# A two-layer trunk on one core: part of product yt4 between the context transposes and the latent kv product, a norm over four transpose banks, sums issued in steps

## The chip, the cores and the metric

The kernel runs on one core of one Trainium2 chip. The metric is the device time of the program in microseconds (us), lower is better. Engines: TensorE does the matmuls (PE) and loads their weights (PEld); VectorE (DVE), ScalarE (ACT) and GpSimd (POOL) work on rows and tiles; SyncE (SP), ACT and POOL also issue DMAs, each on a queue of its own.

## The reference, cut to what matters

A trunk of two layers over 256 latent tokens and 256 context tokens, model width 1024, all in f32. Layer 0 mixes tokens with a bidirectional chunkwise mLSTM, layer 1 with multi-head latent attention in which the latents read context and latents. Behind each mixer follows a gated feed-forward with a depthwise convolution over time. Every sub-layer ends in a LayerNorm and the next begins with a modulation (scale and shift from the condition):

```python
x = _layer_norm(ALPHA * x + ml[2] * yl, ln_g[i, 0], ln_b[i, 0])
f = _conv_ffn(_modulate(x, ml[3], ml[4]), ffn_w_in[i], ffn_conv_w[i], ffn_conv_b[i], ffn_w_out[i])
x = _layer_norm(ALPHA * x + ml[5] * f, ln_g[i, 1], ln_b[i, 1])
...
# latent attention, keys and values, for context (ang None) and latents
ckv, k_rope = jnp.split(h @ w_dkv, [A_KVLORA], axis=-1)
kv = (_rms_norm(ckv, kv_norm) @ w_ukv).reshape(B, T, A_HEADS, A_DNOPE + A_DV)
# queries, for latents only
q = (_rms_norm(h @ w_dq, q_norm) @ w_uq).reshape(B, T, A_HEADS, A_DNOPE + A_DROPE)
```

In layer 1 the context is only read: no output and no feed-forward of the context is computed there.

## The kernel before

**Numbers in two halves.** Every f32 operand is split into a high part in fp32r (an ACT cast) and a low part (a DVE subtraction, operand minus high part). `mm3` (L384 to L386) makes one product of three matmuls: high x high, high x low, low x high. In a product of activations with weights, L385 is the one that reads the low half of the weights, L386 that of the activations.

**The weights' stream.** `Stream` brings all weights in one fixed order, that of `_plan`. `_load` issues the DMA of a weight tile (512 KB at full width) into a ring of buffers called raw, on SP's queue. `_split` makes the ACT cast (L323) and the DVE subtraction (L326). Most halves go to one of three buffers w, and a split waits until PE has released one; weights marked wide go to the large pool u instead (tile wu), and need no release. A raw buffer comes free when its low half is made, and the load that takes its place is issued then.

**The output product of the first feed-forward** (`w_fout0`) is a Strassen-Winograd scheme: seven products of quarter size instead of eight, with sums around them. Four of them, yt2, y11, yt3, yt1, run interleaved over six weight tiles each, into pairs of PSUM banks p6, p1, p7, p5. Then DVE and ACT form the sums of these banks: u2 = p6 + u2 (L1437), p7 = p7 + u2 (L1439), v = p5 - p7 (L1443), p5 = p5 - u2 (L1444), each for two banks. Then y21 accumulates on p1, y22 on p5, yt4 on p7, six weight tiles each, the sixth of half width. The weights of yt4 are made by two transfers: a load from t2d, where sums of other weights have been kept (L278, SP), and on top of it an accumulating DMA from the weights (L279, POOL).

The context rows are complete before yt4. They are normalised (`z_norm`), transposed on PE (`ln_T`, L1197, tile zT), modulated (tile zm, L1204 on ACT, L1206 on DVE) and split (L1209, L1210) into hc, while the first three tiles of yt4 run. Then comes the context's kv product (`mla_ctx`, tile dkv), and then the last three tiles of yt4 (`YTAIL = 3`, marked wide), first for bank 0, then for bank 1. Behind these the latents are normalised the same way, between the context's keys and values (kn, v1).

**Latent attention** (`mla`) begins with the latents' kv product (dkv), the query's down-projection (dq), an rms norm of both (`rms`: square, sqrt and reciprocal, and the scaling L1513 on DVE), transposes, and so on. `ln_x` multiplies the latent rows with gain and bias (L1225, L1226 on DVE) and stores them for the next residual; it waits in the list `late` until `take_late` moves it to the background work.

**The second feed-forward** (layer 1) begins with `after0`: `ln_rows`, then `ln_T`, then the input product (fin). `ln_T` takes one PSUM bank for two of eight 128-column blocks, with both row tiles; of a pair, the first block is modulated by ACT and, where `tail` holds, the second by DVE.

**The order of the work.** Python generators in `bg` hold background work; `tick(n)` runs n steps of it between matmul groups, `drain` the rest. This is the program order; the framework's scheduler then fixes the order on each engine by its own estimate of when operands are ready, except where `keep_in_program_order` pins an instruction. Each engine executes its list in order, and waits on semaphores.

Of the kernel before, what the change touches and what calls it, by code (L numbers as in the profile page):

```python
# [10 lines left out]
AF = mybir.ActivationFunctionType  # L11
ALU = mybir.AluOpType
# [19 lines left out]
NB, NRAW, NU, NS = 3, 3, 31, 15  # L32

SUMS = 5

AHEAD = 8
QA, QB, QC = 2, 4, 6
# [19 lines left out]
YTAIL = 3  # L57
# [13 lines left out]
def _plan():  # L71
    ids, order = {}, []

    def add(key, cols, wide=False):
        if key not in ids:
            ids[key] = (len(ids), cols)
        order.append((key, wide))

    for m in range(16):
        add(("up", m, 0), 1024)  # L80
    for s in range(4):
        for c in range(4):
            add(("og", s, c), 1024)
    for p in range(2):

        for j in range(4):
            for n in ("vt2", "v11", "vt3", "vt1"):
                add((n, p, j), 1024)
        for j in range(4):
            for n in ("v21", "vt4", "v22"):  # L90
                add((n, p, j), 1024)
    add(("gates", 0, 0), 256)
    for h in range(H0):
        for j in range(4):
            for c in range(2):
                add(("qk", (h * 2 + j) if j < 2 else (8 + h * 2 + j - 2), c), 1024)
    for g in range(2):
        for k in range(16):
            add(("mout", 0, k), 1024, g == 1 and k >= 16 - WIDE["mout"])
    for p in range(NF):  # L100
        add(("fin0", p, 0), 1024)
        add(("fin0", p, 1), 1024)
    cols = [1024] * 5 + [512]
    for j in range(6):
        for n in ("yt2", "y11", "yt3", "yt1"):
            add((n, 0, j), cols[j])
    for n in ("y21", "y22", "yt4"):
        for j in range(6):
            if (n, j) == ("yt4", 6 - YTAIL):
                for c, m in enumerate((3, 3, 2)):  # L110
                    add(("dkv", 0, c), m * 320)
            add((n, 0, j), cols[j], n == "yt4" and j >= 6 - YTAIL)
    for c in range(2):
        add(("ukn", 0, c), 1024, True)
    for c in range(2):
        add(("uv", 0, c), 1024, True)
    for c in range(4):
        add(("dq", 0, c), 768)
    for c, n in enumerate((2, 1)):
        add(("uqr", 0, c), n * 512)  # L120
    for c in range(3):
        add(("uqn", 0, c), 1024)
    for k in range(8):
        add(("aout", 0, k), 1024, k >= 8 - WIDE["aout"])
    for p in range(NF):
        add(("fin1", p, 0), 1024, p < 2)
        add(("fin1", p, 1), 1024, p < 2)
    for k in range(NF):
        add(("fout1", 0, k), 1024, k >= NF - WIDE["fout1"])
    return ids, order  # L130
# [224 lines left out]
class K:  # L355
# [830 lines left out]
        nc.vector.tensor_tensor(B, B, sh, op=ALU.add)  # L1186
        return A, B

    def ln_T(self, zs, A, B, dst, tail):

        nc = self.nc
        for kp in range(4):
            pt = self.ps("zT")
            for i in range(2):
                k = kp * 2 + i
                for t in range(2):
                    nc.tensor.transpose(pt[:, i * 256 + t * 128:i * 256 + (t + 1) * 128],  # L1197
                                        zs[t][:, k * 128:(k + 1) * 128], self.ident)
            tmp = self.s2("zm")
            for i in range(2):  # L1200
                k = kp * 2 + i
                c = slice(i * 256, (i + 1) * 256)
                if i == 0 or not tail:
                    nc.scalar.activation(tmp[:, c], pt[:, c], AF.Identity, bias=B[:, k:k + 1], scale=A[:, k:k + 1])  # L1204
                else:
                    nc.vector.tensor_scalar(tmp[:, c], pt[:, c], A[:, k:k + 1], B[:, k:k + 1],  # L1206
                                            op0=ALU.mult, op1=ALU.add)
                hi, lo = dst(k)
                nc.scalar.copy(hi, tmp[:, c])  # L1209
                nc.vector.tensor_sub(lo, tmp[:, c], hi)  # L1210
                if not tail and i == 0:
                    yield
            yield

    def ln_x(self, ln, zs, dst):

# [146 lines left out]
    def w_fout0(self, x1d, mid):  # L1363


        nc, st, A = self.nc, self.st, self.fa
        pin = self.tc.keep_in_program_order
# [4 lines left out]
        def operand():  # L1372
            if parts:
                x, i = parts.pop(0)
                r = self.s2("zr")
                js = [j for j in (2 * i, 2 * i + 1) if j < 11]
                for h, j in enumerate(js):
                    pin(nc.scalar.dma_start(r[:, h * 256:(h + 1) * 256], self.fd[j][:, off[x]:off[x] + 256]))
                got.append((x, js, r))
            if len(got) > 2 or not parts and got:  # L1380
                x, js, r = got.pop(0)
                n = 256 * len(js)
                u = self.u("fz")
                pin(nc.scalar.copy(u[:, 0, :n], r[:, :n]))
                nc.vector.tensor_sub(u[:, 1, :n], r[:, :n], u[:, 0, :n])
                for h, j in enumerate(js):
                    A[x, j] = u[:, :, h * 256:(h + 1) * 256]
# [13 lines left out]
        lo, hi = slice(0, 512), slice(512, 1024)  # L1401
        p6, p1, p7, p5 = [pair() for _ in range(4)]
        n = 0
        u2 = []
        for i in range(6):
            for name, ps, x in (("yt2", p6, "S2"), ("y11", p1, "1"), ("yt3", p7, "S3"), ("yt1", p5, "S1")):
                w = st.use((name, 0, i))
# [8 lines left out]
                if n == 14:  # L1416
                    gate = []
                    for g in (1, 0):
                        t = self.uf("gate")
                        nc.gpsimd.dma_start(t, self.gd[0, 5][g:g + 1, :].to_broadcast([128, 1024]))  # L1420
                        gate.append(t)
                if n >= 16 and n % 2 == 0:
                    if n == 16:
                        z = []
                    t = self.uf("z")
# [7 lines left out]
                        u2.append(u)  # L1433
        stats = [self.tiny(12, "st").rearrange("p (a b) -> p a b", b=6) for _ in range(4)]
        vv = []
        for b in range(2):
            nc.vector.tensor_tensor(u2[b], p6[b], u2[b], op=ALU.add)  # L1437
        for b in range(2):
            nc.vector.tensor_tensor(p7[b], p7[b], u2[b], op=ALU.add)  # L1439
        for b in range(2):  # L1440
            v = self.s2("v")
            nc.scalar.copy(v, p7[b])
            nc.vector.tensor_tensor(v, p5[b], v, op=ALU.subtract)  # L1443
            nc.vector.tensor_tensor(p5[b], p5[b], u2[b], op=ALU.subtract)  # L1444
            vv.append(v)

        def add(g, c, ps, bs=(0, 1)):

            for b in bs:
                t = self.s2("zp")  # L1450
                zz = z[2 * g + b][:, c]
                nc.vector.tensor_tensor(t, ps[b], gate[g][:, c], op=ALU.mult)
                nc.vector.scalar_tensor_tensor(zz, zz, ALPHA, t, op0=ALU.mult, op1=ALU.add)
                nc.vector.bn_stats(stats[2 * g + b][:, c.start // 512], zz)

        def last():
            for b in range(2):
                add(1, hi, vv, (b,))
                yield

        for i in range(6):
            w = st.use(("y21", 0, i))
            prod(p1, "2", w, i, on=True)
            self.tick(1)
            operand()
        add(0, lo, p1)
        self.bg.append(last())
        for i in range(6):
            w = st.use(("y22", 0, i))
# [7 lines left out]
        for i in range(6 - YTAIL):  # L1477
            w = st.use(("yt4", 0, i))
            prod(p7, "3", w, i, on=True)
            self.tick(2)  # L1480
        self.drain()
        mid(None, None, None)
        ws = [(i, st.use(("yt4", 0, i), hold=True)) for i in range(6 - YTAIL, 6)]
        for b in range(2):
            for i, w in ws:
                prod(p7, "3", w, i, (b,), True)
        st.unhold("yt4")
        self.fa = self.fd = None
# [18 lines left out]
    def rms(self, ps, n, dst):  # L1507
        nc = self.nc
        ss = self.tiny(1, "rs")
        nc.scalar.activation(dst, ps, AF.Square, accum_out=ss)  # L1510
        nc.scalar.activation(ss, ss, AF.Sqrt, bias=self.keps, scale=1.0 / n)
        nc.vector.reciprocal(ss, ss)
        nc.vector.tensor_scalar(dst, ps, ss, None, op0=ALU.mult)  # L1513

    def rope_rows(self, out, src, t, n):

# [107 lines left out]
    def mla(self, hl):  # L1624
        nc, st = self.nc, self.st
# [1 line left out]
        rows = self.dkv_rows(self.dkv_mm(hl, self.wd), 2)  # L1627
        self.wd = None
        st.unhold("dkv")
        self.tick()  # L1630
        pss = [self.ps("dq0"), self.ps("dq1")]
        for c in range(4):
            w = st.use(("dq", 0, c))
# [157 lines left out]
def build(tc, off, a, out):  # L1791
    es = ExitStack()
    with es:
        k = K(tc, es, off, a)
        nc = k.nc
# [54 lines left out]
        def after0(pss, xr, gate, g, ln, l, c, dst, xdst):  # L1850
            cond = 1 - g
            A, B = k.ln_mod_cols(ln, l, c, cond)
            yield from k.ln_rows(pss, xr, gate)
            zs = k.zs
            yield from k.ln_T(zs, A, B, dst, g == 1)
            if xdst is not None:
                k.late.append(k.ln_x(ln, zs, xdst))

# [38 lines left out]
        def norm1(g, zs, stats, first):  # L1897
            A, B = k.ln_mod_cols(1, 1, 0, 1 - g)
            if first is not None:
                first()  # L1900
                hlu.extend([k.u("hl") for _ in range(4)])
            yield from k.z_norm(zs, stats)
            yield from k.ln_T(zs, A, B, hl if g else hc, g == 1)
            if g:
                k.late.append(k.ln_x(1, zs, [x2d[0], x2d[1]]))
        k.w_fout0(x1d, mid)
# [8 lines left out]
        k.tick(4)  # L1915
        k.uv((1,))
        k.drain()
        k.take_late()
        att = k.mla(hl)
        oT = next(att)  # L1920
        hl = hlu = None
# [54 lines left out]
```

## Time and profile before

| | |
|---|---|
| median of 3 runs | 1380.56 us (1380.09 to 1381.29) |
| profiled execution: device time | 1379.68 us |
| its span | 1377.9 us |
| granted TensorE clock | 0.998 |
| PE, PEld busy | 1349.8 us (98%), 1121.5 us (81%) |
| DVE, ACT, POOL busy | 1074.9 us (78%), 719.8 us (52%), 121.4 us (9%) |
| HBM read, written | 262.90 MB, 33.46 MB |

The stages that the diff touches lie between 1000 and 1190 us of the span. Where PE pauses there is best read by stage (time stretches of 10 us; busy us and instruction count of each engine, then the granted clock, the mean busy share of the 16 DMA engines, and GB/s):

```profile
1000.00:1010.00 10.00, 8.15 (x35) 5.83 (x34) 10.00 (x15) 8.31 (x12) 0.00 (x0) 1.00 0.90 305
...
1040.00:1050.00 10.00, 9.18 (x59) 7.96 (x58) 6.53 (x21) 9.00 (x22) 3.35 (x5) 1.00 1.04 264
...
1070.00:1080.00 10.00, 8.86 (x51) 7.76 (x52) 9.94 (x23) 7.44 (x19) 0.21 (x1) 1.00 0.00 0
1080.00:1090.00 10.00, 9.04 (x55) 8.69 (x54) 9.49 (x22) 4.96 (x11) 1.96 (x4) 1.00 0.75 241
...
1180.00:1185.00 5.00, 2.63 (x19) 2.01 (x18) 3.72 (x12) 3.11 (x9) 0.00 (x0) 1.00 0.00 0
```

The columns behind the length are PE, PEld, DVE, ACT and POOL. The first row holds the sums of `w_fout0`, the second the context's transposes and its kv product, the third and fourth the latents' transposes, kv product and dq, the last the norm ahead of the second feed-forward. A line of the trace names an instruction by its line, engine, operation and tiles, with the time that its engine sat idle before it and what ended that wait in brackets.

### The profile page before, as it was taken

To read this page: it belongs to the slowest core of one execution; us is meant where nothing else is said; L and a number is where in the kernel's file an instruction comes from. 1 tells how busy PE (TensorE), PEld (TensorE's weight loads), DVE (VectorE), ACT (ScalarE), POOL (GpSimd) and SP (SyncE) were. 2 spreads that over 40 slices of the span, in tenths; PEclk is the share of its full clock that TensorE was granted. 3 is DMA by queue.
4 is the path that set the end of the run, shared out by engine and by line. 5 is a ranking of instruction groups with operands and counts; after the bars stand their busy time and mean duration, and the time that the engine had idled before them with its cause. 6 is when DMAs were issued, how large, how long until landed. Compare 5 with 4: busy or idle time off the path is not lost.

```text
span 1377.9 us, 18614 instructions
## 1 busy us (share of the span) xinstructions
PE 1349.8 (98%) x6583; PEld 1121.5 (81%) x6583; DVE 1074.9 (78%) x1744; ACT 719.8 (52%) x1238; POOL 121.4 (9%) x215
## 2 busy tenths in 40 slices
PE   7999999999999999999999999999999999999997
PEld 3788888888788888878798888888878888888886
DVE  6599757677588696878789977767888889888873
ACT  6585434445544455364644334334557667466660
POOL 0032000011001011120001000000001001000100
PEclk9999999999999999999999999999999999999999
DMA  9689848789666363766747877746887435356760
GB/s 339 232 294 323 284 153 252 236 288 300 215 196 212 108 230 118 255 194 227 234 139 252 291 243 228 220 144 204 304 252 251 150 100 204 111 185 186 253 201 31
DMA packets 97900, 297.58 MB, mean 216 GB/s; under 512 B 12136, under 2 KB 24808, under 8 KB 97808
## 3 DMA queue, kind: packets, MB, share of 16 engines
q1 hardware_dynamic: 68672, 218.52, 48.7%
q0 software_dynamic: 17472, 57.57, 13.2%
q10 hardware_dynamic: 11664, 20.32, 4.1%
q8 instruction: 51, 0.84, 0.3%
q14 instruction: 41, 0.34, 0.1%
HBM read 262.90 MB, written 33.46 MB: 215 GB/s over the span
## 4 chain that ended last, share of the span: by engine, by line
PE 89%; DVE 5%; ACT 2%; DMA 2%; issue 1%; SPq 0%; ACTq 0%; DVEq 0%
PE fin L1318 8%; PE fin L385 6%; PE fin L384 6%; PE fin L386 6%; PE tok L384 6%; PE tok L385 6%; PE tok L386 6%; PE y L385 5%; PE y L386 5%; PE y L384 5%; PE qk L384 4%; PE qk L386 4%; PE qk L385 4%; PE up L384 2%; PE up L386 2%; PE up L385 2%
## 5 line engine op out<-in xcount | busy, mean ns | idle before, releaser
L326 DVE TENSOR_TENSOR w<-raw,w 128x1024 fp32r<-128x1024 f32 (+3 forms) x290 | 348.0, 1202 | 149.0 <-ACT w L323 142.7
L323 ACT CAST w<-raw 128x1024 fp32r<-128x1024 f32 (+3 forms) x290 | 300.3, 1036 | 287.4 <-PE fin L386 78.9
L516 DVE SCALAR_TENSOR_TENSOR junk<-ar,bc 128x1024 f32<-128x1024 f32 x128 | 155.8, 1217 | 4.1 <-ACT bc L558 1.7
L385 PE MATMUL fin<-h,w 128*128 128x512 f32 (+1 forms) x376 | 141.2, 376 | 0.0
L386 PE MATMUL fin<-h,w 128*128 128x512 f32 (+1 forms) x376 | 140.9, 375 | 0.0
L384 PE MATMUL fin<-h,w 128*128 128x512 f32 (+1 forms) x376 | 140.8, 376 | 0.1
L1318 PE MATMUL fin<-h,w 128*128 128x256 f32 (+1 forms) x640 | 112.9, 339 | 0.0
L1318 PEld LDWEIGHTS fin<-h,w 128*128 128x128 f32 x640 | 98.1, 189 | 14.7
L384 PE MATMUL qk<-xc,w 128*128 128x512 f32 x256 | 100.7, 393 | 0.0
L386 PE MATMUL qk<-xc,w 128*128 128x512 f32 x256 | 99.9, 390 | 0.0
L385 PE MATMUL qk<-xc,w 128*128 128x512 f32 x256 | 99.8, 390 | 0.0
L385 PEld LDWEIGHTS fin<-h,w 128*128 128x128 f32 x376 | 70.8, 188 | 13.1 <-DVE h L1210 0.2
L384 PEld LDWEIGHTS fin<-h,w 128*128 128x128 f32 x376 | 70.6, 188 | 13.2 <-ACT h L1209 0.3
L386 PEld LDWEIGHTS fin<-h,w 128*128 128x128 f32 x376 | 70.8, 188 | 12.6
L384 PEld LDWEIGHTS qk<-xc,w 128*128 128x128 f32 x256 | 48.1, 188 | 10.0 <-issue 0.4
L386 PEld LDWEIGHTS qk<-xc,w 128*128 128x128 f32 x256 | 48.1, 188 | 10.0
L385 PEld LDWEIGHTS qk<-xc,w 128*128 128x128 f32 x256 | 48.1, 188 | 9.7
L384 PE MATMUL up<-hT,w 128*128 128x512 f32 x128 | 50.5, 394 | 0.5 <-ACT hT L389 0.5
L385 PE MATMUL up<-hT,w 128*128 128x512 f32 x128 | 50.1, 392 | 0.4 <-DVE hT L390 0.4
L386 PE MATMUL up<-hT,w 128*128 128x512 f32 x128 | 50.1, 391 | 0.3 <-DVE w L390 0.3
L384 PE MATMUL tok<-w,hT 128*128 128x512 f32 x128 | 49.8, 389 | 0.0
L385 PE MATMUL tok<-w,hT 128*128 128x512 f32 x128 | 49.8, 389 | 0.0
(455 smaller groups left out, 3146.4 us busy)
## 6 DMA issues: line engine op xcount, KB each, us to landing
raw<-in_ws SPq DMA_DIRECT2D x287, 512.0 KB, 4.5
ar<-in_adaT SPq DMA_DIRECT2D x80, 512.0 KB, 4.7
adaw<-in_ada_w SPq DMA_DIRECT2D x32, 256.0 KB, 6.7
t2d<-raw ACTq DMA_DIRECT2D x13, 512.0 KB, 6.0
raw<-t2d SPq DMA_DIRECT2D x13, 512.0 KB, 5.7
raw<-in_ws POOLq DMA_DIRECT2D x13, 512.0 KB, 7.8
zr<-fd ACTq DMA_DIRECT2D x33, 128.0 KB, 4.6
xmd<-xr POOLq DMA_DIRECT2D x16, 256.0 KB, 4.6
```

What stands on the lines that cost most here:

```text
L323: k.nc.scalar.copy(h[:, :cols], src)
L326: k.nc.vector.tensor_sub(l[:, :cols], src, h[:, :cols])
L384: mm(out, w[0], x[0], start=start, stop=False, skip_group_check=on)
L385: mm(out, w[0], x[1], start=False, stop=False, skip_group_check=on)
L386: mm(out, w[1], x[0], start=False, stop=stop, skip_group_check=on)
L516: nc.vector.scalar_tensor_tensor(o, w, 1.0, self.bc[j], op0=ALU.mult, op1=ALU.mult, accum_out=col[:, k, j:j + 1])
L1318: nc.tensor.matmul(o, a, b, start=k == 0 and i == 0, stop=k == 7 and i == 1)
```

## The change

The diff has these parts.

- **yt4's fourth tile.** In the plan, tile 3 of yt4 comes ahead of dkv's three tiles. In `w_fout0` its six matmuls for bank 0 are issued before `mid(None, None, None)`, which makes the context's kv product; those for bank 1 stay in the tail.
- **Sums.** The sums behind the four interleaved products become a generator, `sums`, whose steps run between y21's matmul groups, and are drained before y21's result is used.
- **ln_T4.** The norm ahead of layer 1's feed-forward uses four PSUM banks at once: all transposes of row tile 0, five matmuls into a bank that nobody reads (`IDLE`), all transposes of row tile 1. Banks 0 and 2 are modulated by ACT, 1 and 3 by DVE, in the order of the blocks.
- **The norm of layer 0's feed-forward output** (`norm1`) modulates all blocks on ACT (`both=False`).
- **rms** scales on ACT instead of DVE.
- **take_late** moves from ahead of `mla` to behind the latents' dkv rows.

The order on each engine follows from these. On ACT and DVE the changed program has the cast and the subtraction of yt4-3 between those of yt4-0 and yt4-1, and the sums on v and y behind the splits of y21's third to fifth tile; on SP's queue the load of yt4-3 stands ahead of dkv's three loads; POOL's order is unchanged.

```diff
@@ _plan
     for n in ("y21", "y22", "yt4"):
         for j in range(6):
+            add((n, 0, j), cols[j], n == "yt4" and j >= 6 - YTAIL)
             if (n, j) == ("yt4", 6 - YTAIL):
                 for c, m in enumerate((3, 3, 2)):
                     add(("dkv", 0, c), m * 320)
-            add((n, 0, j), cols[j], n == "yt4" and j >= 6 - YTAIL)
@@ ln_T
-    def ln_T(self, zs, A, B, dst, tail):
+    def ln_T(self, zs, A, B, dst, tail, both=True):
...
-                if i == 0 or not tail:
+                if i == 0 or not tail or not both:
                     nc.scalar.activation(tmp[:, c], pt[:, c], AF.Identity, bias=B[:, k:k + 1], scale=A[:, k:k + 1])
@@ new
+    def ln_T4(self, zs, A, B, dst):
+        nc, pin = self.nc, self.tc.keep_in_program_order
+        w = self.st.hl[self.st.nu][0]
+        pts = [self.ps("zT") for _ in range(4)]
+        idle = self.ps("idle")
+        for t in range(2):
+            for k in range(8):
+                o = (k % 2) * 256 + t * 128
+                i = nc.tensor.transpose(pts[k // 2][:, o:o + 128], zs[t][:, k * 128:(k + 1) * 128], self.ident)
+                if t and not k:
+                    pin(i)
+            if not t:
+                for _ in range(IDLE):
+                    pin(nc.tensor.matmul(idle, w[:, 0:128], w[:, 0:512], start=True, stop=True))
+
+        def one(k):
+            c = slice((k % 2) * 256, (k % 2 + 1) * 256)
+            p, m = pts[k // 2][:, c], tmp[:, c]
+            hi, lo = dst(k)
+            if k // 2 % 2 == 0:
+                nc.scalar.activation(m, p, AF.Identity, bias=B[:, k:k + 1], scale=A[:, k:k + 1])
+            else:
+                nc.vector.tensor_scalar(m, p, A[:, k:k + 1], B[:, k:k + 1], op0=ALU.mult, op1=ALU.add)
+            i = nc.scalar.copy(hi, m)
+            nc.vector.tensor_sub(lo, m, hi)
+            return i.ins
+
+        tmp = self.s2("zm")
+        first = one(0)
+        for k in range(1, 8):
+            if k % 2 == 0:
+                tmp = self.s2("zm")
+            with self.tc.issue_after(first):
+                one(k)
+            if k % 2:
+                yield
@@ w_fout0
-        for b in range(2):
-            nc.vector.tensor_tensor(u2[b], p6[b], u2[b], op=ALU.add)
-        for b in range(2):
-            nc.vector.tensor_tensor(p7[b], p7[b], u2[b], op=ALU.add)
-        for b in range(2):
-            v = self.s2("v")
-            nc.scalar.copy(v, p7[b])
-            nc.vector.tensor_tensor(v, p5[b], v, op=ALU.subtract)
-            nc.vector.tensor_tensor(p5[b], p5[b], u2[b], op=ALU.subtract)
-            vv.append(v)
+        def sums():
+            for b in range(2):
+                nc.vector.tensor_tensor(u2[b], p6[b], u2[b], op=ALU.add)
+            yield
+            for b in range(2):
+                nc.vector.tensor_tensor(p7[b], p7[b], u2[b], op=ALU.add)
+            yield
+            for b in range(2):
+                v = self.s2("v")
+                nc.scalar.copy(v, p7[b])
+                nc.vector.tensor_tensor(v, p5[b], v, op=ALU.subtract)
+                nc.vector.tensor_tensor(p5[b], p5[b], u2[b], op=ALU.subtract)
+                vv.append(v)
+                yield
...
+        self.bg.append(sums())
         for i in range(6):
             w = st.use(("y21", 0, i))
             prod(p1, "2", w, i, on=True)
             self.tick(1)
             operand()
+        self.drain()
         add(0, lo, p1)
...
         self.drain()
+        ws = [(6 - YTAIL, st.use(("yt4", 0, 6 - YTAIL), hold=True))]
+        prod(p7, "3", ws[0][1], 6 - YTAIL, (0,), True)
         mid(None, None, None)
-        ws = [(i, st.use(("yt4", 0, i), hold=True)) for i in range(6 - YTAIL, 6)]
+        ws += [(i, st.use(("yt4", 0, i), hold=True)) for i in range(7 - YTAIL, 6)]
         for b in range(2):
-            for i, w in ws:
+            for i, w in ws[1 - b:]:
                 prod(p7, "3", w, i, (b,), True)
@@ rms
-        nc.vector.tensor_scalar(dst, ps, ss, None, op0=ALU.mult)
+        nc.scalar.activation(dst, ps, AF.Copy, scale=ss)
@@ mla
         rows = self.dkv_rows(self.dkv_mm(hl, self.wd), 2)
...
-        self.tick()
+        self.take_late()
@@ build: after0, norm1, ahead of mla
-            yield from k.ln_T(zs, A, B, dst, g == 1)
+            yield from (k.ln_T4(zs, A, B, dst) if l else k.ln_T(zs, A, B, dst, g == 1))
...
-            yield from k.ln_T(zs, A, B, hl if g else hc, g == 1)
+            yield from k.ln_T(zs, A, B, hl if g else hc, g == 1, False)
...
-        k.take_late()
         att = k.mla(hl)
```

More of the change, by code (lines that the diff above doesn't have):

```diff
@@ L34 @@
 SUMS = 5
+IDLE = 5
 AHEAD = 8
```

## The prediction

> **What bounds the kernel now.** I read the page's busy shares and its chain first, then the waits of TensorE (PE) over the whole span, then the timelines around each edit.
>
> ```profile
> PE 1349.8 (98%) x6583; PEld 1121.5 (81%) x6583; DVE 1074.9 (78%) x1744; ACT 719.8 (52%) x1238; POOL 121.4 (9%) x215
> PE 89%; DVE 5%; ACT 2%; DMA 2%; issue 1%; SPq 0%; ACTq 0%; DVEq 0%
> ...
> PE y L385 <- DVE w L326: 2.9, 3, 1.1
> PE zT L1197 <- DVE z L1169: 1.7, 1, 1.7
> PE dq L385 <- DVE w L326: 1.0, 1, 1.0
> PE dkv L384 <- ACT hl L1209: 0.7, 1, 0.7
> PE dkv L386 <- DVE hl L1210: 0.5, 1, 0.5
> ```
>
> The first line is busy time by engine, the second the chain that ended last, by engine; the rest are PE's waits (total, count, longest). PE is busy for 98% and carries 89% of the chain. The change takes no matmul away, so all it can win are waits of PE. Those that it touches are these five lines and two of 0.7 and 0.4 that follow below: 7.9 us together, and one of the three y waits lies elsewhere. What it can lose has no such limit: a cast or subtraction of weights that comes late stops PE. The profiled execution took 1379.68 us (span 1377.9), 0.88 under the median of the runs, 1380.56; I add the difference that I work out to both alike. About 0.2%, 2.8 us, is what a measurement of this kernel tells from no change.
>
> **Sums in steps.** I number the weights of the products, y21-0 to y21-5 and so on.
>
> ```profile
> 1004.64 1.05 ACT L323 CAST w<-raw 128x1024 fp32r<-128x1024 f32 x1
> 1005.77 0.68 DVE L1443 TENSOR_TENSOR v<-y,v 128x512 f32<-128x512 f32 x1
> ...
> 1008.16 1.21 DVE L326 TENSOR_TENSOR w<-raw,w 128x1024 fp32r<-128x1024 f32 x1
> ...
> 1008.07 0.61 PE L384 MATMUL y<-w,fz 128*128 128x512 f32 x2
> 1009.43 0.50 PE L385 MATMUL y<-w,fz 128*128 128x512 f32 x1 [0.74 <-DVE w L326]
> ```
>
> VectorE (DVE) runs four sums between 1005.77 and 1008.16, ahead of the low half of y21-2, whose cast had ended at 1005.69. PE needs that half after the two matmuls of 1008.07, at 1008.5, and gets it at 1009.4. In the changed order this subtraction and two later ones come ahead of the sums: it ends at 1005.77 + 1.21 = 1006.98. Gain 0.9, with the slower restart (0.50 against 0.39) **1.0**. The two additions on u2 keep their places, and so does the longest y wait, of 1.1, behind them. The moved sums are needed by y22, some 10 us later: nothing new is late.
>
> **The moved product.** Six matmuls of yt4-3 now stand around the context transposes. For that yt4-3 is loaded ahead of dkv's three loads on SP's queue, and its cast on ScalarE (ACT) and its subtraction on DVE stand, in the order that the changed program issues, between those of yt4-0 and yt4-1. A yt4 weight takes two transfers, a load from t2d (SP) and behind it an accumulating one (POOL), before it can be cast. When is that for yt4-3?
>
> ```profile
> 1017.09 3.24 SPq L278 DMA_DIRECT2D raw<-t2d  x2
> 1023.53 6.19 SPq L281 DMA_DIRECT2D raw<-in_ws  x3
> 1027.43 0.86 POOL L279 DMA_DIRECT2D raw<-in_ws  x1 [3.59 <-DVE zp L1452]
> raw<-t2d SPq DMA_DIRECT2D x5, 512.0 KB, 6.8
> raw<-in_ws POOLq DMA_DIRECT2D x5, 512.0 KB, 7.9
> 1028.00:1032.00 4.00, 4.00 (x19) 3.31 (x18) 3.77 (x5) 1.05 (x1) 0.29 (x1) 1.00 1.06 284
> 1029.71 1.05 ACT L323 CAST w<-raw 128x1024 fp32r<-128x1024 f32 x1 [2.10 <-PE y L386]
> 1032.43 1.06 ACT L323 CAST w<-raw 128x1024 fp32r<-128x1024 f32 x1 [1.67 <-PE y L386]
> 1035.46 2.05 ACT L323 CAST w<-raw 128x1024 fp32r<-128x1024 f32 x2 [1.97 <-DMA raw<-in_ws]
> ```
>
> The two rows with KB are DMA issues around this stage, with the median time to landing. The three ACT rows are the casts of yt4-0, yt4-1 and yt4-2 (with dkv's first). yt4-2 shows the rhythm: loaded at 1020.0 (the second of the two issues from 1017.09 on), landed after 6.8, accumulated from 1027.43 (0.6 later), landed after 7.9 at 1035.3; its cast at 1035.46 waited for just that. yt4-3 takes the place of dkv's first load, 1023.53, which frees up 1.0 earlier by the gain above: 1022.5. Then 1022.5 + 6.8 + 0.6 + 7.9 = **1037.8**. The DMA engines are full in that stretch (share 1.06), so I take these medians and not the fastest landings. ACT works in its order: yt4-1's cast, due at 1032.43 - 1.0 = 1031.4, waits behind yt4-3's until 1038.8.
>
> On DVE, yt4-1, yt4-2, dkv and the whole context norm are queued behind yt4-3's subtraction:
>
> ```profile
> 1030.80 1.23 DVE L326 TENSOR_TENSOR w<-raw,w 128x1024 fp32r<-128x1024 f32 x1 [0.23 <-ACT w L323]
> 1033.11 0.69 DVE L1452 TENSOR_TENSOR zp<-y,gate 128x512 f32<-128x512 f32 x1 [1.09 <-PE y L386]
> 1033.72 1.22 DVE L326 TENSOR_TENSOR w<-raw,w 128x1024 fp32r<-128x1024 f32 x1
> 1034.85 0.69 DVE L1453 SCALAR_TENSOR_TENSOR z<-z,zp 128x512 f32<-128x512 f32 x1
> 1042.04 2.25 PE L1197 MATMUL zT<-ident,z 128*128 128x128 f32 x16
> 1044.98 0.42 PE L384 MATMUL dkv<-w,hc 128*128 128x320 f32 x1 [0.68 <-ACT hc L1209]
> 1038.80 0.39 PE L386 MATMUL y<-w,fz 128*128 128x512 f32 x1
> 1041.52 0.39 PE L386 MATMUL y<-w,fz 128*128 128x512 f32 x1
> ```
>
> From a cast's start to its subtraction it is 1.09 (1029.71 to 1030.80); from a subtraction to the next instruction 1.13 (1033.72 to 1034.85); from zp at 1033.11 to the first transpose at 1042.04 it is 8.93, and DVE has no pause in it that the delay could use up. So the transposes start 11.15 after yt4-3's cast, at 1048.95: **6.9 late**. PE's own work lies inside that: a weight is 12 matmuls, 2.72 (1038.80 to 1041.52), yt4-1 gets its low half at about 1041.9, and yt4-2 ends near 1047.7. The delay disappears only if the cast starts by 1029.7, which is 1037.8 less the 6.9 and the 1.0 of the sums, and a little.
>
> What the move is paid with: six matmuls are 1.36, and the wait of 0.68 ahead of dkv, 0.8 with its restart, takes that much of them. PE gets back **0.8**.
>
> ```profile
> 1052.15 0.39 PE L384 MATMUL y<-wu,fz 128*128 128x512 f32 x1
> 1059.68 0.28 PE L384 MATMUL kn<-ckT,wu 128*128 128x256 f32 x1
> ```
>
> From dkv's end to kn there were 7.5 us, in which 30 matmuls of yt4 hid the rms chain. Now 24 do, and that chain's scaling moves to ACT, behind two wide casts. If the chain gets no shorter, this costs the whole 1.36; if it fits, nothing. I take **0.3**, nearer to nothing, since 24 matmuls are still 5.4 us.
>
> **The latent stage.**
>
> ```profile
> 1073.13 0.68 DVE L1225 TENSOR_TENSOR z<-z,gr 128x512 f32<-128x512 f32 x1
> 1073.61 2.57 ACT L1209 CAST hl<-zm 128x256 fp32r<-128x256 f32 x8
> 1083.42 0.44 PE L385 MATMUL dq<-w,hl 128*128 128x384 f32 x1 [0.96 <-DVE w L326]
> ```
>
> All eight zm go to ACT, and the passes over z (L1225 and L1226, 0.6 each, eight of them) go behind the dkv rows. In before, hl's casts start at 1073.61 behind all zm, and DVE's low halves behind a z pass. In the changed order four casts come ahead of the last four zm. Both dkv waits, 0.7 + 0.5, lose their cause: **1.2**. ACT keeps up afterwards: about 0.5 for a zm and 0.3 for a cast per k, against 6 matmuls of 320 columns, some 0.85. The dq weight no longer stands behind z passes: **1.0**. In exchange six of these passes, 3.6, stand ahead of the query rows' reciprocals; 48 kn matmuls of half y's width, some 5.5, cover them, and without cover they cost 3.6. I take **0.3**, bounds 0 and 1.0. The x2d stores on POOL come later, with 80 us in hand.
>
> **The second feed-forward's norm.**
>
> ```profile
> 1182.45 1.57 PE L1197 MATMUL zT<-ident,z 128*128 128x128 f32 x12 [1.71 <-DVE z L1169]
> 1183.04 1.05 ACT L1204 ACTIVATE zm<-zT,lnB,lnA 128x256 f32<-128x256 f32 x2 [0.27 <-PE zT L1197]
> 1183.64 1.03 DVE L1206 TENSOR_SCALAR zm<-zT,lnA,lnB 128x256 f32<-128x256 f32 x2 [0.78 <-ACT zm L1204]
> 1184.43 0.74 PE L384 MATMUL fin<-h,wu 128*128 128x256 f32 x4 [0.40 <-ACT h L1209]
> ```
>
> The wait of 1.71 is for the norm itself and stays. Behind it come 8 transposes instead of 12; the first h is cast behind one zm, not two (0.5 sooner); and DVE has banks of its own instead of waiting 0.78 for ACT's zm. Gain **0.5**, bounds 0 and 0.9. The five idle matmuls, 5 x 0.227 = 1.1, and four more transposes, 0.4, fit into the 1.71; without that cover they would cost 1.1.
>
> **Sum.** 6.9 - 0.8 + 0.3 - 1.2 - 1.0 + 0.3 - 0.5 = **+4.0 us** (the 1.0 of the sums is already in the 6.9): 1383.7 for a profiled execution, **1384.6** against the median.
>
> **Rivals.**
> 1. *Faster: yt4-3 lands before ACT reaches it.* Point: a cast by 1029.7. Then the 6.9 becomes -1.0, and the sum is -3.9: 1376.7. For it speaks only that a short transfer would do; load and accumulation would need 3.3 each, against 6.8 and 7.9. The Trainium skill, "DMA: Bandwidth & Descriptors", section "Anatomy of one DMA", gives a transfer from POOL 2.0 us plus bytes over 436e3, by my estimate 3.2 us for 512 KB; by that rule this rival would hold, and these rows speak against it. Chance 0.14.
> 2. *It lands early, but not in time.*
>
> ```profile
> DMA to landing us min/median/max: 5.5/7.8/12.5
> DMA to landing us min/median/max: 4.6/5.7/6.8
> ```
>
> These are all accumulations (first) and t2d loads of the run. With 5.5 and 4.6 the cast is at 1033.2, 4.6 sooner: -0.6, 1380.0, no change that can be measured. Chance 0.13. With 12.5 it is 4.6 later, 1389.2.
> 3. *PE comes back slow.* It idles from about 1035.3 to 1039.8. If the 22 matmuls then left of yt4-1 and yt4-2 ran at twice their 0.227, they would end at 1041.9 + 10.0 = 1051.9, 2.9 past the transposes' time: 1387.5. Before has no such idle stretch, and behind the 1.71 fin was not slowed. The Trainium skill, "TensorE: Matmul & The Clock Gate", section "What's actually happening", has the clock halved after an idle window of about 3.4 us. Chance 0.07.
>
> **Numbers.** The forecast itself has 0.66, and I put 0.06 of that under +0.2%. The range 1379.0 to 1389.0 holds it with its landing bounds and rivals 2 and 3; rival 1 is left out. Faster 0.14, same 0.19, slower 0.67.
>
> **What would show it.** Right: on ACT a wait of 5 us or more for a transfer ahead of a wu cast near 1037; PE idle for some 6 us in yt4-1; context transposes near 1049; no v or y sum ahead of y21-2; no waits of dkv and dq in the latent stage; fin sooner behind its transposes. Wrong: yt4-1 cast within 2 us of yt4-0, the transposes before 1044, or a span under 1377.

## The result, and the profile after

The changed kernel takes 1385.15 us (median of 6 runs, 1384.31 to 1386.80) against 1379.95 for the kernel before on the same chip (6 runs, 1378.93 to 1381.29): ratio 1.0039, 95% interval 1.0028 to 1.0050. The forecast was 1384.6. The profiled execution spans 1382.5 us against 1377.9, 4.6 more.

The page's busy line and chain first, then PE's waits over the whole span (total, count, longest):

```profile
PE 1353.8 (98%) x6588; PEld 1124.1 (81%) x6588; DVE 1070.5 (77%) x1734; ACT 723.1 (52%) x1248; POOL 121.0 (9%) x215
PE 89%; DMA 4%; DVE 3%; ACT 2%; issue 2%; ACTq 0%; SPq 0%; DVEq 0%; POOLq 0%
```

```profile
PE y L386 <- ACT w L325: 5.5, 2, 5.3
PE y L387 <- DVE w L328: 3.4, 3, 1.3
...
PE s L386 <- ACT qn L1753: 0.6, 1, 0.6
```

The shares hide it: PE is still 98% busy. But DMA now holds 4% of the chain, one wait of PE for a cast is 5.3, and the waits of dkv and dq are gone from the list. In their place stands one of the scores (s) for qn. Stretch by stretch (PE, PEld, DVE, ACT, POOL, then granted clock, DMA share, GB/s):

```profile
1030.00:1040.00 10.00, 5.48 (x25) 4.20 (x23) 1.25 (x2) 1.30 (x2) 0.00 (x0) 0.99 0.95 260
1040.00:1050.00 10.00, 8.01 (x25) 6.00 (x25) 9.77 (x16) 5.62 (x8) 1.73 (x2) 0.67 0.80 200
1070.00:1080.00 10.00, 10.00 (x63) 8.60 (x62) 7.74 (x21) 7.10 (x19) 0.00 (x0) 1.00 0.26 80
1080.00:1090.00 10.00, 9.99 (x64) 9.73 (x65) 7.45 (x16) 8.37 (x21) 0.00 (x0) 1.00 0.24 76
```

From 1030 to 1040 DVE and ACT stand nearly still with the DMA engines almost full, and from 1035.5 on PE too. The latent stage, where PE had been busy 8.86 and 9.04 of 10, has no gap left. The timeline at the standstill, ACT, DVE and PE:

```profile
1028.71 1.05 ACT L325 CAST w<-raw 128x1024 fp32r<-128x1024 f32 x1 [2.10 <-PE y L388]
1038.70 1.04 ACT L325 CAST wu<-raw 128x1024 fp32r<-128x1024 f32 x1 [8.93 <-DMA raw<-in_ws]
1039.65 2.88 ACT L325 CAST w<-raw 128x1024 fp32r<-128x1024 f32 x3
1039.78 1.22 DVE L328 TENSOR_TENSOR wu<-raw,wu 128x1024 fp32r<-128x1024 f32 x1 [8.75 <-ACT wu L325]
1040.92 0.68 DVE L1498 TENSOR_TENSOR zp<-y,gate 128x512 f32<-128x512 f32 x1
1049.56 0.54 DVE L1552 TENSOR_SCALAR z<-z,mv,rs 128x512 f32<-128x512 f32 x1
1040.74 0.79 PE L386 MATMUL y<-w,fz 128*128 128x512 f32 x1 [5.27 <-ACT w L325]
1045.51 0.63 PE L387 MATMUL y<-w,fz 128*128 128x512 f32 x1
1050.16 0.44 PE L1199 MATMUL zT<-ident,z 128*128 128x128 f32 x2
```

ACT waits 8.93 for yt4-3 (the wu), then casts three weights in a row that had been ready. DVE waits with it, and the pass zp of the context norm, which needs nothing of yt4-3, comes after. The context transposes start at 1050.16 instead of 1042.04.

The table gives the start of the first matmul of each stage: for before in us of the span, for the others the difference to before. It includes three experiments that are explained below.

| first matmul of | before | after | e4 (move alone) | e1 (order) | f1 (behind the norm) |
|---|---|---|---|---|---|
| y21 | 1001.12 | +0.02 | -0.44 | -0.12 | +0.27 |
| context transposes | 1042.04 | +8.12 | +8.13 | +0.65 | +0.08 |
| context dkv | 1044.98 | +8.19 | +8.21 | +2.95 | +1.04 |
| kn | 1059.68 | +6.88 | +7.62 | +1.48 | +0.58 |
| latent dkv | 1074.09 | +5.77 | +6.66 | +0.51 | -0.39 |
| qr | 1098.97 | +4.23 | +8.40 | -1.00 | -1.88 |
| scores | 1113.38 | +4.79 | +8.39 | -0.45 | -1.33 |
| attention's output product | 1153.50 | +5.25 | +8.44 | -0.04 | -0.92 |
| fin | 1184.43 | +4.81 | +8.45 | -0.48 | -1.36 |
| last matmul | 1369.88 | +4.65 | +8.46 | -0.63 | -1.50 |

So 8.1 is lost at the transposes, 3.9 of it won back by qr, 1.0 lost again in the attention, and 0.6 won at the second norm.

Each column is a single execution. Six kernels below (f1, f3, f4, g1, g2, g4) have the same order on ACT and DVE between y21 and the transposes, and yet their executions take 39.18 to 42.72 for that stretch. A difference of one or two us there between two columns is therefore no effect of an edit; the 8.1 is.

### The profile page after: what moved, and what is told of

Its sections match the earlier page's. It is cut to its first block, busy times and chain, and to the rows that moved or that the text cites. A ratio compares the mean times of both kernels' runs of the same rounds, so it can differ in the third digit from the quotient of the medians.

```text
span 1382.5 us, 18613 instructions
## 1 busy us (share of the span) xinstructions
PE 1353.8 (98%) x6588; PEld 1124.1 (81%) x6588; DVE 1070.5 (77%) x1734; ACT 723.1 (52%) x1248; POOL 121.0 (9%) x215
## 4 chain that ended last, share of the span: by engine, by line
PE 89%; DMA 4%; DVE 3%; ACT 2%; issue 2%; ACTq 0%; SPq 0%; DVEq 0%; POOLq 0%
PE fin L1359 8%; PE fin L386 6%; PE fin L387 6%; PE fin L388 6%; PE tok L386 6%; PE tok L388 6%; PE tok L387 6%; PE y L387 4%; PE y L388 4%; PE y L386 4%; PE qk L386 4%; PE qk L388 4%; PE qk L387 4%; DMA raw<-in_ws 2%; PE up L386 2%; PE up L387 2%
## 5 line engine op out<-in xcount | busy, mean ns | idle before, releaser
L328 DVE TENSOR_TENSOR wu<-raw,wu 128x1024 fp32r<-128x1024 f32 (+1 forms) x33 | 39.2, 1202 | 17.8 <-ACT wu L325 17.5
L386 PE MATMUL tok<-w,hT 128*128 128x512 f32 x128 | 49.9, 390 | 0.0
```

The costliest lines, as they stand in the source:

```text
L328: k.nc.vector.tensor_sub(l[:, :cols], src, h[:, :cols])
L386: mm(out, w[0], x[0], start=start, stop=False, skip_group_check=on)
```

## Experiments

**e1: yt4-3 behind yt4-2 on ACT and DVE.**

```diff
@@ Stream._split
-        src = raw[:, :cols]
+        src, pin = raw[:, :cols], k.tc.keep_in_program_order if key == ("yt4", 0, 3) else lambda i: i
...
-            k.nc.scalar.copy(h[:, :cols], src)
+            pin(k.nc.scalar.copy(h[:, :cols], src))
-            k.nc.vector.tensor_sub(l[:, :cols], src, h[:, :cols])
+            pin(k.nc.vector.tensor_sub(l[:, :cols], src, h[:, :cols]))
```

> The changed kernel, with the cast and the subtraction of yt4-3 pinned behind those of yt4-2 on ACT and DVE; transfers and matmuls as they were. Theory (yt4-3 stands ahead of yt4-1 on two queues and lands late): yt4-1's cast comes back to about 1031.4, PE's wait of 5.3 in yt4-1 is gone, the context transposes start between 1041 and 1044 (the subtraction of 1.2 still stands ahead of a part of the norm), and the time falls by 8.1 less 0 to 2: 1377 to 1379. Rival (the late part is the transfers: dkv's loads have lost a place on SP's queue, and the DMA engines are full): the order on ACT and DVE is no matter, and the time stays over 1382.

Measured: 1380.55 against 1379.60, ratio 1.001 (1.000 to 1.002). The timeline of e1, ACT's casts of yt4-1, yt4-2 and yt4-3, then PE:

```profile
1030.55 1.05 ACT L325 CAST w<-raw 128x1024 fp32r<-128x1024 f32 x1 [1.75 <-DMA raw<-in_ws]
1033.82 1.05 ACT L325 CAST w<-raw 128x1024 fp32r<-128x1024 f32 x1 [2.22 <-DMA raw<-in_ws]
1037.23 1.05 ACT L325 CAST wu<-raw 128x1024 fp32r<-128x1024 f32 x1 [2.35 <-DMA raw<-in_ws]
1042.69 1.06 PE L1199 MATMUL zT<-ident,z 128*128 128x128 f32 x4 [2.29 <-DVE z L1552]
1043.97 0.63 PE L386 MATMUL y<-wu,fz 128*128 128x512 f32 x1
```

The 5.3 is gone and the transposes start at 1042.69 with the same transfers: the order was the loss, not the queue of dkv's loads. The time fell less than expected: against the kernel before, 5.2 of loss became 1.0. In the trace the square roots of the norm now stand behind this cast on ACT, PE waits 2.29 ahead of the transposes, and the matmuls after it run slowly (0.63 for one instead of 0.39).

**e2: the changed kernel, yt4-3 without its accumulating transfer** (this tile's weights lack their second part; the other tiles have it).

```diff
@@ Stream._load
-            k.nc.gpsimd.dma_start(t[:, :cols], self.ws[n, :, :cols], accum_op=ALU.add)
+            key == ("yt4", 0, 3) or k.nc.gpsimd.dma_start(t[:, :cols], self.ws[n, :, :cols], accum_op=ALU.add)
```

> The changed kernel without the accumulating transfer of yt4-3 (that tile's weights lack their second part); order on ACT and DVE as in the changed kernel. Theory: yt4-3 is complete with its first load, which lands by about 1028 (its accumulation was issued at 1026.8), so ACT meets it without a wait behind yt4-0's cast, and the order costs only the 1.0 and 1.2 of the cast and the subtraction themselves: transposes between 1041 and 1043, time 1376.5 to 1378.5. Rival (dkv's loads, or the additional engine work): dkv's loads and all work on the engines are the same, so the time stays over 1382.

Measured: 1377.40 against 1379.60, ratio 0.9983 (0.9974 to 0.9993). In its timeline the cast that stood at 1038.70 is at 1025.98:

```profile
1025.98 1.06 ACT L325 CAST wu<-raw 128x1024 fp32r<-128x1024 f32 x1 [0.31 <-DMA raw<-t2d]
1042.94 0.44 PE L1199 MATMUL zT<-ident,z 128*128 128x128 f32 x2 [0.82 <-DVE z L1552]
```

The order did not stay quite as expected: DVE's is that of the changed kernel, but on ACT this cast now stands one place further ahead still, before that of yt4-0 (1027.77). With the late landing away, even that does no harm. This is the prediction's first rival made true, and the change is then faster than before by 2.2, where that rival's sum was 3.9. The edit also takes 512 KB off the DMA engines; what that alone is worth was not tested.

**e3: everything but the moved product; e4: the moved product alone.** Both are the plan's line and the six matmuls of `w_fout0` of the diff above, taken back in the changed kernel and put into the kernel before.

> The changed kernel with yt4-3 back behind dkv in the plan and its six matmuls back in the tail; all other edits stay. Theory: the moved product is the whole loss, and what is left are gains: sums -1.0, dkv in the latent stage -1.2, dq and its follow-up -1.5, ln_T4 -0.6, against +1.0 that the attention lost: -3.3, 1376.7. Rival (other edits lose too, as the new wait of the scores on ACT suggests): 1379 or more.

> The kernel before, with the moved product alone (its place in the plan, its six matmuls around the context transposes). Theory: the same late landing, without the 1.0 that the sums give: transposes near 1051, of which 1.3 comes back by kn, so +7 to +8: 1387 to 1388. Rival (the loss needs the other edits as well): under 1384.

Measured: e3 1378.07, ratio 0.9992 (0.9982 to 1.0001); e4 1391.95 (1388.11 to 1394.17), ratio 1.0093 (1.0071 to 1.0114). The moved product is the whole loss, as expected, but both sizes are off: the rest gives 1.5 and not 3.3, the move alone costs 8.5 in the profiled execution, and 12 in the median of four. The profiled execution is the fastest of the four, with a granted clock of 0.996 over its span; the others have 0.992 to 0.993, and no trace shows where they lost it. The table shows why for e4: the 1.5 that comes back by the latent dkv is lost again by qr. Two waits of its latent stage, from the list of PE's waits:

```profile
PE ckT L1563 <- DVE ckr L1515: 2.0, 1, 2.0
...
PE dq L385 <- DVE w L326: 0.7, 1, 0.7
```

On DVE the passes of `ln_x` over z stand ahead of the rms reciprocals there. So the edits of the latent stage matter more beside the moved product: from kn to qr they take 3.4 off e4 (40.07, changed kernel 36.64), and 1.7 off the kernel before (39.29, e3 37.58).

**f1: yt4-3 behind the context norm.** Its cast is queued behind the norm's second square root, its subtraction behind the second pass over z.

```diff
@@ z_norm, second row tile
+                for late, first in zip(self.y3, (sq, zp)):
+                    self.tc.add_manual_dep(late.ins, first.ins.name, mybir.DependencyInfo(
+                        mybir.DependencyClass.NoSync, mybir.DependencyReason.DATA), reason="norm first")
```

> The changed kernel, with the cast of yt4-3 queued on ACT behind the square roots of the context norm, and its subtraction on DVE behind the norm's passes over z (instead of ahead of yt4-1). Theory: pinned behind yt4-2 it still stood ahead of the norm: an ACT wait of 2.35 for the landing, then the norm's square roots, a PE wait of 2.3 ahead of the transposes, and eight matmuls at nearly double pitch. Here nothing of the norm is queued behind the transfer: PE's wait ahead of the transposes is under 1, no slow matmuls, and 3 us are won against the order behind yt4-2: 1376 to 1377. Rival (the six matmuls now wait for their own late halves, and dkv behind them): the waits only move, and the time stays at 1379 to 1381.

Measured: 1378.16 against 1380.12, ratio 0.9987 (0.9978 to 0.9996). The timeline, ACT and PE:

```profile
1042.36 1.03 ACT L325 CAST wu<-raw 128x1024 fp32r<-128x1024 f32 x1
1042.12 1.60 PE L1202 MATMUL zT<-ident,z 128*128 128x128 f32 x10 [0.64 <-DVE z L1555]
```

The cast waits for nothing, PE's wait ahead of the transposes is 0.64, no matmul is slow. The change becomes faster than before. The expected 3 us against e1 are there in the medians: e1 is 1.0 over before, f1 2.0 under it. The two profiled executions differ by 0.9 only; that of e1 (1379.13) is among the fastest of its ten (1379.02 to 1382.91), and PE loses 0.9 in that of f1 ahead of kn, waiting for ckr and ckT, with only 24 matmuls of yt4 behind dkv. This loss is not there in every execution: f4 and g1, which have the same order on ACT and DVE up to kn, take 13.36 and 13.35 from dkv to kn, f1 14.24, before 14.70.

**Parts of the latent edits, on f1.** f3 puts take_late back ahead of mla; g2 puts the scaling of rms back on DVE; g4 gives DVE every second zm again.

```diff
@@ f3: mla, build
-        self.take_late()
+        self.tick()
...
+        k.take_late()
         att = k.mla(hl)
@@ g2: rms
-        nc.scalar.activation(dst, ps, AF.Copy, scale=ss)
+        nc.vector.tensor_scalar(dst, ps, ss, None, op0=ALU.mult)
@@ g4: norm1
-            yield from k.ln_T(zs, A, B, hl if g else hc, g == 1, False)
+            yield from k.ln_T(zs, A, B, hl if g else hc, g == 1)
```

> The previous kernel (yt4-3 behind the norm), with take_late back ahead of mla. Theory: the scores' new wait (0.8 for qn on ACT) comes from the last passes over z, which stand ahead of the query's rope on DVE since take_late was moved; here it goes, and dq's wait of 1.0 for its low half comes back: within 0.4 of the previous kernel. Rival (the scores' wait comes from the rms scaling on ACT): it stays, and dq's is added: 1.0 slower.

> The kernel with yt4-3 behind the norm (five idle matmuls kept), with the scaling of rms back on DVE. Theory: on DVE the scaling stands behind passes over z and casts' subtractions, so kn and the query transposes get their input later: 0.5 to 1.5 slower than with ACT. Rival (either engine has room): the same within 0.3, and the edit is worth nothing.

> The kernel with yt4-3 behind the norm (five idle matmuls kept), with every second modulation of the latents (zm) back on DVE. Theory from the prediction: the two waits of dkv, 1.2, come back. Rival (the moved product had already taken most of them, as the kernel with the move alone shows, 0.5 left of 1.4): 0.3 to 0.5 slower.

Measured: f3 1381.99, ratio 1.0017 (1.0008 to 1.0026), 3.8 slower than f1; g2 1382.87 against 1379.51, ratio 1.0024 (1.0015 to 1.0032), so 3.4 over before where f1 was 2.0 under it; g4 1378.34, ratio 0.9987 (0.9978 to 0.9995), as f1. One line of each, f3 and g4 from the list of PE's waits, g2 from its timeline:

```profile
PE ckT L1619 <- ACT ckr L1571: 3.5, 3, 1.8
```

```profile
1093.57 0.58 PE L390 MATMUL kn<-ckT,wu 128*128 128x256 f32 x1 [2.35 <-DVE ckT L1624]
```

```profile
PE dkv L391 <- DVE hl L1215: 0.3, 1, 0.3
```

In f3 the scores' wait did go, as expected, but the passes over z stand ahead of the reciprocals: PE waits 3.5 ahead of ckT (3.3 of it in the latent stage), not 1.0 at dq. In g2 six passes, 3.6 us of DVE, stand ahead of ckT's low half, which PE needs for kn, and 14 of the kn matmuls from that wait on take 0.41 or more instead of 0.28. Both losses are larger than either expectation allowed (1.0 and 1.5 at most). Both edits are needed together. The zm edit is worth the 0.3 that the wait shows: the moved product had taken the rest of dkv's waits by itself (e4 has 0.3 left of 1.2), and so do the other edits without it (e3, 0.3).

**g3: sums in one piece, on f1** (the generator's body back in line ahead of y21).

> The kernel with yt4-3 behind the norm (five idle matmuls kept), with the sums in one piece ahead of y21 as in the kernel before. Theory from the prediction: PE's stall of 0.9 at 1008 is back, 1.0 slower throughout. Rival: the context norm on DVE sets the transposes, and DVE's work is the same in either order, so half of it or less: 0 to 0.5.

Measured: 1377.11 against 1379.51, ratio 0.998 (0.9971 to 0.9988). Its stall is back, and the medians show no cost:

```profile
1009.28 0.50 PE L390 MATMUL y<-w,fz 128*128 128x512 f32 x1 [0.72 <-DVE w L328]
```

g3 is 2.4 under before where f1 was 2.0 under it, so the medians speak for the rival (0 to 0.5) and leave little room for 1.0. The traces can't tell: from y21 to the transposes g3 takes 41.27, inside the 39.18 to 42.72 of the kernels that have the sums in steps. That DVE's norm sets the transposes, so that its work in either order is the same, fits PE's wait of 0.48 for z ahead of them, but is argued.

**c1: PE kept busy in the changed kernel's standstill.** 42 matmuls between yt4-0 and yt4-1 (one ahead of the loop shown; the trace has 39 of them), with the order elsewhere held, as far as it bears on the norm, by dependences that only order.

```diff
@@ w_fout0, behind yt4-0
+                for _ in range(41):
+                    pin(nc.tensor.matmul(idle[:, 0:256], A["3", 0][:, 0, 0:128], A["3", 0][:, 0], start=True, stop=True))
```

> The changed kernel, with 39 matmuls of 256 columns (4.7 us, into a bank that nobody reads) in PE's idle time between yt4-0 and yt4-1; order on ACT, DVE, SP and POOL held as in the changed kernel as far as it bears on the norm. Theory (the slow clock was hidden, DVE's pass over z at 1049.6 sets the transposes): yt4-1 and yt4-2 run at pitch 0.227 again and end 1.5 to 2 earlier, the transposes stay within 0.5 of 1050.2, and the time is that of the changed kernel, 5 over before. Rival (the slow clock set the transposes): they come 1.8 earlier, and the time is 3.4 over before.

Measured: 1384.83, ratio 1.0036 (1.0026 to 1.0046), the changed kernel's. PE in its timeline:

```profile
1034.30 4.83 PE L1536 MATMUL idle<-fz 128*128 128x256 f32 x39
1039.58 0.49 PE L390 MATMUL y<-w,fz 128*128 128x512 f32 x1 [0.44 <-ACT w L325]
...
1049.53 0.66 PE L1203 MATMUL zT<-ident,z 128*128 128x128 f32 x4 [1.05 <-DMA raw<-in_ws]
```

No matmul is slow (granted clock 1.00 from 1030 to 1050), and PE waits for the norm instead. Two transposes start at 1047.87, since the first pass over z is ahead of a subtraction of dkv here, but the rest stand behind a wait of 1.05. The line names a transfer; DVE's second pass over z ends at 1049.36, just before the transposes go on. From yt4-3's cast (1037.53 here, 1038.70 in the changed kernel) to the context's dkv it is 14.74, against 14.47. In the changed kernel the slow clock was hidden behind DVE.

**f4: f1 without the five idle matmuls** (`IDLE = 0`).

> The first kernel of this set without the five idle matmuls of ln_T4. Theory: the wait of PE for the norm ahead of the second feed-forward is the norm's own time, and its 1.9 of idling did not slow fin in the kernel before: fin starts within 0.2, the time is the same within 0.5. Rival (the idle matmuls keep the clock up): the first matmuls of fin run at double pitch, 1 us or more slower.

Measured: 1377.88, ratio 0.9985 (0.9976 to 0.9994), as f1. But its profiled execution shows what the idle matmuls can be for:

```profile
1179.92 1.24 PE L1230 MATMUL zT<-ident,z 128*128 128x128 f32 x8 [1.49 <-DVE z L1174]
...
1182.23 0.42 PE L390 MATMUL fin<-h,wu 128*128 128x256 f32 x1
```

After an idle wait of 1.49 the first matmuls of fin take 0.42 instead of 0.28; the first hundred take 13.81 instead of 12.33 in f1. The next kernel, g1, has no idle matmuls either and the same wait of 1.49, and its hundred take 12.32. So the slow clock comes in some executions, and the median shows no cost.

**g1: f4 with the casts of the last two uqn weights behind the first qn on ACT.**

```diff
@@ queries
+            for c in self.cast[1:] if i == 0 else ():
+                self.tc.add_manual_dep(c.ins, a.ins.name, mybir.DependencyInfo(
+                    mybir.DependencyClass.NoSync, mybir.DependencyReason.DATA), reason="qn first")
```

> The kernel with yt4-3 behind the norm and no idle matmuls, and the casts of the second and third uqn weights queued on ACT behind the first scaling of qn. Theory: what is left of the scores' wait (0.8 for qn on ACT) is these casts standing ahead of qn; it goes, and the time is 0.5 to 1 lower than without this edit, 1377, below before by 2.5 to 3. Rival (the weights are then late for the next qn): the wait moves to qn's matmuls, and nothing is won.

Measured: 1377.31 against 1379.51, ratio 0.9983 (0.9974 to 0.9991). The scores' wait is gone from PE's list, and from qn to the attention's output product it takes 44.98 instead of f1's 45.77 (before 44.80). Against before this is 2.2 faster, against f4, also 2.2 faster than before, nothing that the medians show.

## Why the prediction was right, step by step

**The late transposes (6.9, measured 8.1).** The mechanism is shown from two sides: the same transfers with the cast further back (e1, f1), and the cast as far ahead without the late transfer (e2). The landing was right by compensation. The load was taken at 6.8 and had landed when its accumulation was issued, 4.2 after it; the accumulation was taken at 7.9, the median, and took 11.9 (issued 1026.79, cast at 1038.70). In e1 three accumulations, issued at 1023.12, 1024.33 and 1025.63, are complete by 1030.55, 1033.82 and 1037.23, when the casts that wait for them start: as if one behind another, 3.3 to 3.4 apart. The step to price was yt4-3's place in that queue, not a median. The place alone does not fix the landing, though: in e2, with two in the queue, the first took 9.5 (1023.44 to 1032.93), and the second came 3.8 later. So the cast came at 1038.70 instead of 1037.8, and from it to the transposes it was 11.46 instead of 11.15; together they make the 1.2. The Trainium skill, "DMA: Bandwidth & Descriptors", section "Anatomy of one DMA", gives 3.2 for 512 KB by my estimate, 2.0 plus the bytes. The spacing in e1 is near that, whether for its reason or not; as a landing time it is short by more than 8 here.

**The sums (1.0, no gain found).** Mis-sized. The stall of PE at 1008 did go, and yt4-3's load was issued at 1022.54, as worked out. But e4, without the edit of the sums, issued this load at 1022.27 and cast yt4-3 at 1038.77: in its execution the stall behind y21's first matmuls was 0.4 and not 1.1, so the early load is not shown to be the sums' doing, and the landing did not follow it. Where yt4-3 is out of the way, the medians show no gain (g3). The term was read off PE's gap without asking what is late next.

**The moved product's return (-0.8 and +0.3, measured -1.3).** From context dkv to kn the lag falls by 1.31, about the six matmuls (1.36): the shorter cover cost nothing in the changed kernel. Where the norm is early it depends on the execution: 0.46 comes back in f1, with an excess of 0.9 ahead of kn, and 1.34 and 1.35 in f4 and g1.

**The latent stage (-1.2, -1.0 and +0.3, measured -2.65 from kn to qr).** The direction held, the size was 0.75 short, and the attribution did not hold. Beside the moved product the zm edit removes only 0.3 of the dkv waits (g4); why the moved product removes the rest was not settled. The dq step is right in the changed kernel, but take_late and rms hang together with the move: taking either back beside it costs 4 to 5 (f3, g2). The 0.3 for z passes ahead of the reciprocals was not paid: in the changed kernel three of the four pairs of passes run from 1096.6 to 1100.3 without a wait of PE.

**Not predicted: +1.0 in the attention.** In the changed kernel's order the second rope on DVE starts 4.55 behind the first (1107.69, 1112.24), in before 2.35 (1102.76, 1105.11). So qn on ACT stands behind a late qrs, and the scores wait. From qn to the attention's output product e1, e2, e3 and f1 have the same excess of nearly 1.0 (45.76 or 45.77, before 44.80); e4 (44.85), f3 (44.80) and g1 (44.98) do not, and in these three the second rope stands as early ahead of qn's first matmul as in before (3.60) or earlier, in f1 0.69. f3 differs from f1 only in the place of take_late, so that edit brings the wait.

**The second norm (-0.5, measured -0.6).** Right: fin comes 0.45 sooner against the transposes, and its first hundred matmuls take 0.16 less. The idle matmuls are hidden in the wait, as said.

**The rivals.** The first became true only in e2. The third was half right: PE did come back slow, at a pitch of 0.427, but its price was not paid in the profiled execution, since DVE was later (c1).

**The total.** The last matmul starts 4.65 later than in before, against the +4.0 of the forecast. The transposes came 1.2 later than worked out and the attention added 1.0, against 0.8 more by kn, 0.75 more in the latent stage and 0.1 more at the second norm. The sign and the main term follow from the mechanism; that the total came so close is in part luck.

## What to carry to other kernels

A weight that needs no free buffer has no natural place in an engine's queue: if the order rests on an estimate of its landing, it can be put ahead of work that is due much earlier, and the whole queue then waits for one transfer. Order such a cast behind the work that is due first (here a loss of 5.2 us became a gain of 2), and price a landing by what is queued ahead of it. A stall that disappears counts only as far as the next engine in the chain is not the later one, and edits that share a queue have to be priced together.

## What the hardware showed

Accumulating transfers of 512 KB on POOL's queue completed 3.3 to 3.4 apart with the DMA engines full (share 1.01 from 1024 to 1037 in e1), though they were issued 1.2 to 1.3 apart. In f1 two of them completed 3.2 apart, in e2 3.8, by the casts that waited for them.

The granted clock fell to 0.50 from 1040 to 1045 in the changed kernel after 5.27 of idling; seven matmuls ran at a pitch of 0.427 instead of 0.227, and the full pitch was back 5.9 after PE resumed. In e1 a wait of 2.29 and the four transposes behind it were enough for 0.81 there, in f4 a wait of 1.49 between two rows of eight transposes for 0.72 from 1180 to 1184, and in g2 a wait of 2.35 among kn's matmuls, with no transpose beside it, for 0.64 from 1094 to 1098:

```profile
1040.00:1045.00 5.00, 3.00 (x6) 2.11 (x7) 5.00 (x7) 3.81 (x4) 1.54 (x2) 0.50 0.61 129
```

```profile
1040.00:1045.00 5.00, 2.71 (x10) 1.84 (x9) 4.19 (x10) 4.09 (x7) 1.11 (x2) 0.81 0.84 181
```

```profile
1180.00:1184.00 4.00, 3.71 (x21) 3.31 (x22) 3.34 (x9) 3.81 (x11) 0.00 (x0) 0.72 0.00 0
```

```profile
1094.00:1098.00 4.00, 4.00 (x24) 4.00 (x24) 2.96 (x7) 0.41 (x2) 0.20 (x1) 0.64 0.73 278
```

The first is the changed kernel, the second e1, the third f4, the fourth g2. The Trainium skill, "TensorE: Matmul & The Clock Gate", section "What's actually happening", has the clock halved after an idle window of about 3.4. The changed kernel agrees; the other three show it after shorter waits, and g1 shows no drop (1.00 from 1180 to 1184) after the same wait as f4.
